# A hybrid encoder layer on one NeuronCore: new tables for the order of the instructions

## The chip, the cores and the metric

The kernel runs on 1 core of a Trainium2 chip. The core has five engines, each with an instruction stream of its own that it works off strictly in order: TensorE (PE in the rows: matmuls and transposes), VectorE (DVE), ScalarE (ACT), GpSimd (POOL) and SyncE (SP), which here only starts the DMAs. An engine whose next instruction waits for another engine stands still, with all that is queued behind that instruction.

The metric is the device time of one execution in microseconds (us). Lower is better.

## The reference

One encoder layer is computed for a prompt of 1024 frames and for the next 64 frames of a running stream that has a cache of 512 frames. Only the order of the operations matters here; all of it is float32.

```
z = x @ w_in                      # split into q,k,v,f of 6 FoX heads, u,v of the SGU, q,k,v of 6 stick-breaking heads
# A  FoX: causal softmax attention, logit += c_t - c_s with c = cumsum(log_sigmoid(f))
p = softmax(where(mask, q k^T / 8 + c_q - c_k, -1e30));  o_fox = p v
# B  SGU: 128-frame chunks, w_s lower triangular per channel group
u = gelu(u_g); v = layer_norm(gelu(v_g));  o_sgu = u * (w_s v + b_s)
# C  stick-breaking, strictly causal
a = exp(log_sigmoid(z) + sum of log_sigmoid(-z) over the later keys);  o_sb = a v
o = rms_norm_per_head(concat(o_fox, o_sgu, o_sb)) * g_mix
x = layer_norm(ALPHA * x + o @ w_out)
h = square(relu(x @ w_up));  y = layer_norm(ALPHA * x + h @ w_down)     # d_model 1024, d_ff 4096
```

The outputs are y for both groups and the new rows of the caches.

## The kernel before

**Matmuls in three passes.** A float32 matmul is made of three passes of a rounded type: each operand is split into a high part (a copy on ACT) and a low part (`lo_sub`, L215: source minus high part, on DVE or POOL), and `PASSES=((0,0),(0,1),(1,0))` multiplies high by high, high by low and low by high into one PSUM bank. Every tile that goes into a matmul therefore passes through ACT and then through DVE or POOL. Rows of L215 are such low parts, whatever the tile.

**Stage 1, to about 540 us: projection and attention.** `fill` makes the projections (L495, tiles kvfox, kvsb, sgv, sgu, qfox, qsb) and the SGU; `attn` makes the attention blocks. The build interleaves the two by a running cost. For a block of FoX heads the scores Sfox (L696) get the bias on DVE (L668) and the exponential on ACT. For stick-breaking the scores Ssb go through two sigmoids on ACT (L678, L679), a running product along the keys on DVE (L680, a scan of up to 1024 columns) and a product on POOL (L682, sgsb). PE transposes the rows (L744, ptfox and ptsb), ACT and DVE split them into high and low (pthfox, pthsb; L712 and L215), and PE multiplies them by v (L754 to L757, ofox and osb; L754 and L755 use the high part, L756 and L757 the low part). The SGU's v goes through a GELU (L893 to L896: ACT, DVE, ACT, DVE; tiles g1v and sgvv) and a LayerNorm (L967 to L973), and is mixed over 128 frames (L943, sgm). sgv and sgm share a ring of two PSUM banks, so a matmul of sgm waits until L896, the last reader of an older sgv, is done.

**Stage 2, to about 700 us:** the heads are normed (L316, L317), and the output projection (L373, mx) and the first LayerNorm follow; transposes (L1322, xta to xtd) make the MLP's operand xo.

**Stage 3, about 660 to 1000 us: x @ w_up** as a Winograd-like scheme: for each of 16 pieces p of w_up and for each of two column groups s (288 and 256 columns), seven products of 12 matmuls each (L1448) in four PSUM banks per s, zA, zB, zC and zD, three of the products in zA. After each product in zA, ACT copies the bank out (L1459, sn), and the next product into zA adds onto what is there; it has to wait for that copy. DVE makes the sums, relu and square (L1462 to L1492, hh), which go to DRAM. The weights are prepared beside it: load (wr), high parts (wa on ACT, L1386), low parts on POOL (L215), sums on DVE (L1395 to L1399), the sums' high parts on ACT (L1669, ws, two copies of 128x1024 for a piece) and low parts on DVE.

**Stage 4, from about 1000 us: h @ w_down** in the same scheme with 512 columns (L1913, banks A, B, D and p), the sums on DVE (L1878 and L1880, tiles acc), weights rd and wd split on ACT, POOL and DVE, and a LayerNorm at the end (L1982 to L2026).

**What sets the order.** The order in which an engine runs its instructions is not that of the code. At the end of `_build` (L2269 to L2283) a table for each of PE, ACT, DVE and POOL is read: a word `n+k` (n is 1 and k is 0 where left out) means n times "take the instruction with number k of those of this engine that are not yet taken". Each instruction taken gets an order dependency, without a semaphore, on the one taken before it. So a table is a permutation of the engine's instructions. SP has no table before: the order of its 672 DMAs comes from `in_order` helpers in a few places and from the scheduler.

Of the kernel before, what the change touches and what calls it, by code (L numbers as in the profile page):

```python
# [48 lines left out]
ORDER = {}  # L49
ORDER["PE"] = """  # L50
# [43 lines left out]
"""  # L94
ORDER["ACT"] = """
# [2208 lines left out]
```

## Time and profile before

| | |
|---|---|
| median of 3 runs | 1355.06 us (1354.13 to 1358.22) |
| profiled execution, its own time | 1357.01 us |
| profiled execution, span from first to last instruction | 1355.3 us |
| mean granted clock of TensorE | 0.991 of full speed |
| instructions | 24318 |
| PE busy | 1298.2 us, 96% of the span, 8827 matmuls and transposes |
| DVE / ACT / POOL busy | 1000.4 / 719.7 / 620.4 us |
| longest group on PE | 103.4 us, the output projection, 416 matmuls |

In the rows, a line reads: start, duration, engine, line of the code, operation, tile written <- tiles read (buffer numbers left out), shape, and in brackets the time that the engine stood idle before it and what ended that. Rows of a table by stretch give, for each engine, busy microseconds and the number of instructions in brackets, then the granted clock of TensorE and the use of the DMA engines. PE counts as busy while a matmul runs at half clock.

### The profile page before, as it was taken

The numbers are of one execution on the slowest core, as the hardware profiler recorded it, in microseconds if no ns is written. First come the engines' busy times: TensorE is split into PE (matmuls) and PEld (weight loads), VectorE is DVE, ScalarE is ACT, GpSimd is POOL, SyncE is SP. The second block draws the span as 40 slices with busy tenths as digits, with TensorE's granted clock in tenths as the row PEclk, the third lists the DMA queues.
The fourth block names the chain that finished last, engine by engine and source line by source line (L and its number), as shares of the span: only waits on it lengthen the run. The fifth ranks groups of instructions, "written<-read, shape, count | busy, mean of one in ns | idle before, by whom it ended". The sixth has DMA issues, their size and how long they took to land.

```text
span 1355.3 us, 24318 instructions
## 1 busy us (share of the span) xinstructions
PE 1298.2 (96%) x8827; PEld 1184.7 (87%) x8827; DVE 1000.4 (74%) x1797; ACT 719.7 (53%) x1561; POOL 620.4 (46%) x666
## 2 busy tenths in 40 slices
PE   7999999999999998999999999999999999999996
PEld 7898989999988997787899999999986888877774
DVE  4577666576888389779886777877687776767787
ACT  4366666576656376334523232232267676767665
POOL 3222222255675457666512221212186665655657
PEclk9999999999999998999999999999999999999998
DMA  7435565141403257432234444344568344434343
GB/s 230 110 117 149 157 201 146 53 101 44 101 16 77 63 180 260 147 117 70 79 120 143 157 139 160 127 153 149 189 231 280 125 143 149 144 121 160 102 140 132
DMA packets 158048, 185.64 MB, mean 137 GB/s; under 512 B 27740, under 2 KB 116124, under 8 KB 157928
## 3 DMA queue, kind: packets, MB, share of 16 engines
q1 hardware_dynamic: 155832, 183.01, 42.3%
q8 instruction: 70, 1.15, 0.4%
q10 hardware_dynamic: 2096, 1.07, 0.3%
q14 instruction: 50, 0.41, 0.1%
HBM read 117.65 MB, written 60.10 MB: 131 GB/s over the span
## 4 chain that ended last, share of the span: by engine, by line
PE 30%; DVE 8%; POOL 6%; DMA 5%; ACT 4%; issue 2%; SPq 0%; DVEq 0%; POOLq 0%; ACTq 0%
PE zA L1448 9%; PE zD L1448 6%; PE A L1913 4%; PE zB L1448 3%; PE zC L1448 3%; POOL wd L215 3%; PE D L1913 2%; DMA rd<-w_down 2%; POOL rd L1580 2%; PE mx L373 1%; DMA awa<-h_dr 1%; PE B L1913 1%; ACT wd L1386 1%; ACT st L1611 1%; DMA hs_dr<-hh 1%
## 5 line engine op out<-in xcount | busy, mean ns | idle before, releaser
L215 POOL TENSOR_TENSOR wa<-wr,wa 128x512 fp32r<-128x512 f32 x41 | 61.2, 1518 | 216.1 <-ACT wa L1386 216.1
L215 POOL TENSOR_TENSOR wd<-rd,wd 128x512 fp32r<-128x512 f32 x77 | 101.0, 1323 | 105.3 <-ACT wd L1386 68.1
L373 PE MATMUL mx<-xT,oTb 128*128 128x512 f32 (+1 forms) x416 | 103.4, 400 | 2.6 <-DVE oTb L215 2.4
L1448 PE MATMUL zD<-xo,ws 128*128 128x288 f32 (+1 forms) x720 | 95.2, 286 | 0.3 <-DVE hh L1462 0.3
L1448 PE MATMUL zA<-xo,ws 128*128 128x288 f32 (+1 forms) x720 | 95.0, 286 | 0.0
L373 PEld LDWEIGHTS mx<-xT,oTb 128*128 128x128 f32 (+1 forms) x416 | 75.7, 188 | 20.6 <-DVE oTb L215 3.7
L1448 PEld LDWEIGHTS zD<-xo,ws 128*128 128x128 f32 x720 | 91.5, 188 | 0.5 <-DVE hh L1462 0.5
L1448 PEld LDWEIGHTS zA<-xo,ws 128*128 128x128 f32 x720 | 91.4, 188 | 0.1
L495 PE MATMUL kvfox<-wkvfox,xT 128*128 128x256 f32 (+3 forms) x624 | 88.0, 289 | 3.2 <-ACT wkvfox L471 3.0
L1580 POOL TENSOR_TENSOR rd<-rd 128x512 f32<-128x512 f32 x56 | 79.2, 1415 | 23.8 <-DVE b L215 21.5
L1386 ACT ACTIVATE wd<-rd 128x512 fp32r<-128x512 f32 x105 | 63.6, 623 | 45.9 <-POOL rd L1580 23.9
L495 PE MATMUL kvsb<-wkvsb,xT 128*128 128x256 f32 (+1 forms) x624 | 87.2, 285 | 0.2 <-ACT wkvsb L471 0.2
L682 POOL TENSOR_TENSOR sgsb<-sgsb,snsb 128x127 f32<-128x127 f32 (+7 forms) x48 | 59.5, 1242 | 57.9 <-DVE snsb L680 47.8
L1913 PE MATMUL A<-wd,wd 128*128 128x512 f32 x312 | 82.4, 393 | 2.4 <-DVE acc L1880 1.9
L495 PEld LDWEIGHTS kvfox<-wkvfox,xT 128*128 128x128 f32 (+1 forms) x624 | 79.5, 190 | 4.7 <-ACT wkvfox L471 3.4
L680 DVE TENSOR_TENSOR_SCAN snsb<-snsb,one 128x128 f32<-128x128 f32 (+7 forms) x48 | 72.0, 1502 | 10.9 <-ACT snsb L679 9.3
L495 PEld LDWEIGHTS kvsb<-wkvsb,xT 128*128 128x128 f32 (+1 forms) x624 | 78.2, 187 | 0.6 <-ACT wkvsb L471 0.4
L1913 PEld LDWEIGHTS A<-wd,wd 128*128 128x128 f32 x312 | 57.8, 188 | 17.9 <-DVE acc L1880 4.3
L1459 ACT ACTIVATE sn<-zA 128x256 f32<-128x256 f32 (+1 forms) x80 | 30.9, 388 | 68.4 <-PE zA L1448 60.9
L1913 PE MATMUL A<-wd,h4a 128*128 128x512 f32 x240 | 64.1, 392 | 1.8 <-DVE acc L1880 1.0
L1669 ACT ACTIVATE ws<-wr 128x1024 fp32r<-128x1024 f32 x28 | 29.1, 1056 | 64.3 <-DVE wr L1398 64.3
L1386 ACT ACTIVATE wa<-wr 128x512 fp32r<-128x512 f32 x42 | 23.5, 622 | 61.6 <-DMA wr<-w_up 57.7
(551 smaller groups left out, 3765.7 us busy)
## 6 DMA issues: line engine op xcount, KB each, us to landing
h_dr<-hh SPq DMA_DIRECT2D x30, 512.0 KB, 3.2
rd<-w_down SPq DMA_DIRECT2D x30, 512.0 KB, 4.5
wr<-w_up SPq DMA_DIRECT2D x13, 1024.0 KB, 5.5
hr<-h_dr SPq DMA_DIRECT2D x31, 384.0 KB, 4.1
h_dr<-hh SPq DMA_DIRECT2D x30, 384.0 KB, 3.6
raw<-w_in SPq DMA_DIRECT2D x44, 256.0 KB, 3.2
wo_dr<-swo SPq DMA_DIRECT2D x32, 256.0 KB, 2.3
xT<-wo_dr SPq DMA_DIRECT2D x8, 1024.0 KB, 7.9
```

Of the source, the lines that this page charges most:

```text
L215: eng.tensor_tensor(out, src, hi.bitcast(F32), op=ALU.subtract)
L373: nc.tensor.matmul(acc[0:m], oT[:, k, hx, 0:m], wo[k // 4][hw][:, k % 4, cs], start=(i == 0), stop=(i == len(seq) - 1))
L495: nc.tensor.matmul(acc[0:n, c0:c0 + n1 - n0], xT[k // 4][:, k % 4, c:c + n], wt[:, k, hw, n0:n1], start=(i == 0), stop=(i == len(seq) - 1))
L680: nc.vector.tensor_tensor_scan(g[:, 0:n][:, ::-1], g[:, 0:n][:, ::-1], one.broadcast_to([P, n]), 1.0, op0=ALU.mult, op1=ALU.bypass)
L682: nc.gpsimd.tensor_tensor(s[:, 0:n - 1], s[:, 0:n - 1], g[:, 1:n], op=ALU.mult)
L1386: nc.scalar.activation(hi, raw, AF.Copy)
L1448: nc.tensor.matmul(z, w[:, hw, k], xop(s, bo, hx)[:, k, :], start=(new and k == 0 and j == 0), stop=(k == 3 and j == 2), skip_group_check= ...
L1459: nc.scalar.activation(c, z, AF.Copy)
L1580: eng.tensor_tensor(r[:, o], r[:, x], r[:, y], op=ALU.subtract)
L1611: nc.scalar.activation(st, t[:, 0, q].bitcast(F32), AF.Copy)
L1669: nc.scalar.activation(ws[:, 0, q, c], src[:, q], AF.Copy)
L1913: nc.tensor.matmul(z, h[:, hx, q, o], wset[self.c % 2][q][:, hw, wb], start=((n in (0, 3) or n == 1 and self.c == 0) and q == 0 and j == 0 ...
```

## The change

The tables of PE, ACT, DVE and POOL are replaced by others, a table for SP is added, and the loop that reads them takes SP too and leaves out instructions that only mark a boundary. Nothing else changes: each engine has the same instructions with the same operands, and SP's new table gives the same order of DMAs as before. The new tables add 88 lines, so that L1448 before is L1536 after, L215 is L303, L896 is L984, and lines from L163 on shift alike. The number of runs of equal rows in PE's order goes from 2939 to 4166: the new order changes between tiles more often.

```diff
 ORDER["PE"] = """
-9 8+23 55 +8 8+25 +8 14 4+34 2+10 45 4+1 7+13 1 +12 4+36 12 4+24 14 2+36 19 15+1 8 8+24 24 +8 8 8+1 9 8+1
...
++4 2 2+2 4 2+23 +25 4+23 12 4+12 2+32 +11 2+31 6 +5 +24 2+5 +51 2 +20 2+51 7+3 2+13 3 +39 +36 8 +10 2 +25 +51
...
+ORDER["SP"] = """
++9 +4 1 +20 +38 1 2+39 +4 +6 +37 +8 +36 +38 +263 4 2+14 10 2+4 4 4+19 1 4+1 +10 2+1 6 2+38 1 +2 1 6+1 4 +2 1
...
-    for eng, e in (("PE", nc.tensor), ("ACT", nc.scalar), ("DVE", nc.vector), ("POOL", nc.gpsimd)):
-        left = [i for i in traced[from_here:] if i.engine == e.engine]
+    for eng, e in (("PE", nc.tensor), ("ACT", nc.scalar), ("DVE", nc.vector), ("POOL", nc.gpsimd), ("SP", nc.sync)):
+        left = [i for i in traced[from_here:] if i.engine == e.engine and "Boundary" not in type(i).__name__]
         prev = None
         for word in ORDER[eng].split():
             n, k = (int(x or d) for x, d in zip(re.match(r"(\d*)\+?(\d*)", word).groups(), (1, 0)))
```

Three places show what the new tables do. The names carry the block and a running number: sgvv5 is the SGU's v of row tile 5, zA2_0 is bank A for weight piece 2 and column group 0.

The first is on DVE, near 400 us, where the SGU and stick-breaking run side by side. Before:

```order
L680 SCALAR_TENSOR_TENSOR snsb1_5_1_5694<-snsb1_5_1_5694,one_70 128x768
L971 TENSOR_SCALAR sgvv4_5777<-sgvv4_5777,sgst4_5783 128x256
L894 SCALAR_TENSOR_TENSOR g1v5_5819<-g1v5_5819,sgv5_5793 128x256
L972 TENSOR_TENSOR sgvv4_5777<-sgvv4_5777,gvb_5432 128x256
L896 TENSOR_TENSOR sgvv5_5818<-g1v5_5819,sgv5_5793 128x256
L215 TENSOR_TENSOR pthsb1_2_0_2_5713<-ptsb1_2_0_2_5709,pthsb1_2_0_2_5713 128x384
```

After, from the same scan to the same split (L303 is L215 before, L768 is L680, L982 is L894, L1059 is L971, L984 is L896, L1060 is L972):

```order
L768 SCALAR_TENSOR_TENSOR snsb1_5_1_5694<-snsb1_5_1_5694,one_70 128x768
L982 SCALAR_TENSOR_TENSOR g1v5_5819<-g1v5_5819,sgv5_5793 128x256
L1059 TENSOR_SCALAR sgvv4_5777<-sgvv4_5777,sgst4_5783 128x256
L984 TENSOR_TENSOR sgvv5_5818<-g1v5_5819,sgv5_5793 128x256
L1060 TENSOR_TENSOR sgvv4_5777<-sgvv4_5777,gvb_5432 128x256
L303 TENSOR_TENSOR pthsb1_2_0_2_5713<-ptsb1_2_0_2_5709,pthsb1_2_0_2_5713 128x384
```

The GELU's two steps for tile 5 (g1v5 and sgvv5) have each moved ahead by one LayerNorm step of tile 4.

The second is on DVE, near 532 us, in the last stick-breaking block, from its scan to the second low part of its rows. Before:

```order
L680 SCALAR_TENSOR_TENSOR snsb2s_7666<-snsb2s_7666,one_70 128x576
L997 TENSOR_TENSOR up6_7231<-up6_7231,sgu7_1_7685 128x256
L316 TENSOR_REDUCE ss0_7568<-sq0_7566 128x8
L894 SCALAR_TENSOR_TENSOR g1u5_7629<-g1u5_7629,up4_7162 128x256
L317 SCALAR_TENSOR_TENSOR ss0_7568<-ss0_7568,rge_7560 128x8
L215 TENSOR_TENSOR pthsb2_3_1_0_7700<-ptsb2_3_1_0_7695,pthsb2_3_1_0_7700 128x512
L997 TENSOR_TENSOR up8_7262<-up8_7262,sgu8_1_7732 64x256
L316 TENSOR_REDUCE ss0_7568<-sq0_7566 128x8
L776 TENSOR_REDUCE otsb2_3_0_7703<-otpsb2_3_0_7704 128x2x64
L502 TENSOR_TENSOR up8_7262<-up8_7262,sgu8_1_7732 64x256
L215 TENSOR_TENSOR pthsb2_3_1_1_7713<-ptsb2_3_1_1_7708,pthsb2_3_1_1_7713 128x512
```

After (L404 is L316, L405 is L317):

```order
L768 SCALAR_TENSOR_TENSOR snsb2s_7666<-snsb2s_7666,one_70 128x576
L404 TENSOR_REDUCE ss0_7568<-sq0_7566 128x8
L405 SCALAR_TENSOR_TENSOR ss0_7568<-ss0_7568,rge_7560 128x8
L303 TENSOR_TENSOR pthsb2_3_1_0_7700<-ptsb2_3_1_0_7695,pthsb2_3_1_0_7700 128x512
L404 TENSOR_REDUCE ss0_7568<-sq0_7566 128x8
L982 SCALAR_TENSOR_TENSOR g1u5_7629<-g1u5_7629,up4_7162 128x256
L405 SCALAR_TENSOR_TENSOR ss0_7568<-ss0_7568,rge_7560 128x8
L303 TENSOR_TENSOR pthsb2_3_1_1_7713<-ptsb2_3_1_1_7708,pthsb2_3_1_1_7713 128x512
```

The up6 product has moved behind, g1u5 from ahead of pthsb2_3_1_0 to between it and pthsb2_3_1_1, and the up8 steps and the reduction of otsb2_3_0 behind both.

The third is on PE, in stage 3, from the end of the second product of piece 2 in zA2_0 to its third. Before:

```order
L1448 MATMUL zA2_0_9410<-xo0_8042,ws2_9350 128x288 x12
L1448 MATMUL zA2_1_9424<-xo13_8811,ws2_9350 128x256 x12
L1448 MATMUL zD2_0_9492<-xo0_8042,ws2_9350 128x288 x12
L1448 MATMUL zD2_1_9505<-xo14_8810,ws2_9350 128x256 x12
L1448 MATMUL zA2_0_9410<-xo0_8042,ws2_9350 128x288 x12
```

After:

```order
L1536 MATMUL zA2_0_9410<-xo0_8042,ws2_9350 128x288
L1536 MATMUL zC2_1_9560<-xo13_8811,wa2_9261 128x256
L1536 MATMUL zA2_0_9410<-xo0_8042,ws2_9350 128x288
L1536 MATMUL zC2_0_9546<-xo0_8042,wa2_9261 128x288
L1536 MATMUL zD2_0_9492<-xo0_8042,ws2_9350 128x288
L1536 MATMUL zA2_0_9410<-xo0_8042,ws2_9350 128x288 x2
L1536 MATMUL zD2_0_9492<-xo0_8042,ws2_9350 128x288 x2
L1536 MATMUL zC2_0_9546<-xo0_8042,wa2_9261 128x288
L1536 MATMUL zD2_0_9492<-xo0_8042,ws2_9350 128x288 x2
L1536 MATMUL zC2_0_9546<-xo0_8042,wa2_9261 128x288
L1536 MATMUL zA2_0_9410<-xo0_8042,ws2_9350 128x288 x12
L1536 MATMUL zA2_1_9424<-xo13_8811,ws2_9350 128x256 x2
```

Before, whole products of 12 matmuls lie between the second and the third product in zA2_0, 36 matmuls in all; after, products are cut into short runs, and 6 matmuls lie between them.

Elsewhere the moves are of the same kind and size: tiles of PE's order move by a few microseconds of PE's work, in stage 3 by up to nine. In stage 4, at about 1030 us, DVE's second split of wd1_0 moves behind the sums of D1_0 and A1_1, and the sum of A1_0 ahead of that of p11_0. At about 431 us, DVE's split pthsb1_3_0_3 moves ahead of g1v8 (L894). Near 57 us, PE's first scores Sfox2 move behind projection matmuls of kvfox1_1 and qfox2_2.

More of the change, by code (lines that the diff above doesn't have):

```diff
@@ L50 @@
 ORDER["PE"] = """
[43 rows of a table removed]
[104 rows of a table added]
 """
 ORDER["ACT"] = """
[25 rows of a table removed]
[31 rows of a table added]
 """
 ORDER["DVE"] = """
[31 rows of a table removed]
[36 rows of a table added]
 """
 ORDER["POOL"] = """
[6 rows of a table removed]
[11 rows of a table added]
+"""
+ORDER["SP"] = """
[9 rows of a table added]
 """
```

294 rows, old and new, of the table ORDER are left out of this document.

## The prediction

> **What bounds the kernel now.** I read the page's busy line first, then the stretches, then the chain of work, then PE's waits, and last what DVE and ACT were doing at those waits.
>
> ```profile
> PE 1298.2 (96%) x8827; PEld 1184.7 (87%) x8827; DVE 1000.4 (74%) x1797; ACT 719.7 (53%) x1561; POOL 620.4 (46%) x666
> PE 30%; DVE 8%; POOL 6%; DMA 5%; ACT 4%; issue 2%; SPq 0%; DVEq 0%; POOLq 0%; ACTq 0%
> ```
>
> PE is busy for 1298.2 of 1355.3 us, and no other engine exceeds 74%. An order changes no amount of work, so what it can win or lose is PE's idle 57.1 us and the time that PE ran at half clock. In the chain that ended last, PE leads with 30%, and DVE (8%), POOL (6%) and DMA (5%) follow. By stretches (length, busy us of PE, its weight loads, DVE, ACT, POOL, then granted clock and DMA):
>
> ```profile
> 0.00:700.00 700.00, 660.88 (x4953) 618.76 (x4954) 508.95 (x1030) 388.19 (x920) 324.07 (x427) 0.99 0.41 121
> 700.00:1000.00 300.00, 300.00 (x2423) 299.12 (x2423) 225.11 (x340) 93.84 (x179) 70.68 (x47) 1.00 0.46 154
> 1000.00:1355.30 355.30, 337.37 (x1454) 266.79 (x1452) 266.32 (x429) 237.68 (x463) 225.62 (x193) 0.99 0.45 154
> ...
> 70.00:74.40 4.40, 3.94 (x22) 3.82 (x21) 3.85 (x12) 3.21 (x10) 1.04 (x2) 0.61 0.67 179
> 401.00:406.00 5.00, 3.98 (x19) 3.53 (x20) 3.42 (x10) 3.82 (x9) 2.94 (x5) 0.66 0.13 28
> 432.00:437.00 5.00, 4.91 (x28) 4.61 (x29) 3.81 (x10) 3.69 (x9) 2.39 (x4) 0.66 0.58 130
> 534.00:543.00 9.00, 7.54 (x32) 6.42 (x33) 8.65 (x18) 4.11 (x9) 7.31 (x7) 0.62 0.98 369
> ```
>
> Of the idle time 39.1 us lie before 700 us, none between 700 and 1000, and 17.9 after. So stage 3 has nothing to give and can only lose. The last four rows show the clock: length times (1 minus clock) is 1.7, 1.7, 1.7 and 3.4 us, 8.5 us of work lost.
>
> The large waits on PE (in brackets the idle time and what ended it):
>
> ```profile
> 4.44 0.87 PE L451 MATMUL xtp<-ident,xr 128*128 128x128 f32 x3 [4.44 <-DMA xr<-x_prompt]
> 57.00 0.58 PE L696 MATMUL Sfox<-kpfox,qdfox 128*128 128x128 f32 x3 [1.67 <-DMA qdfox<-qdfox]
> 401.50 0.38 PE L943 MATMUL sgm<-vh,wst 128*128 128x256 f32 x1 [1.75 <-DVE sgvv L896]
> 431.92 0.33 PE L756 MATMUL osb<-pthsb,vpsb 128*128 128x128 f32 x1 [1.67 <-DVE pthsb L215]
> 534.62 0.38 PE L756 MATMUL osb<-pthsb,vpsb 128*128 128x256 f32 x1 [2.25 <-DVE pthsb L215]
> 1029.66 0.96 PE L1913 MATMUL A<-wd 128*128 128x512 f32 x3 [1.23 <-DVE acc L1878]
> 1032.03 0.94 PE L1913 MATMUL A<-wd,h4a 128*128 128x512 f32 x3 [0.72 <-DVE acc L1880]
> 1034.00 0.49 PE L1913 MATMUL D<-wd 128*128 128x512 f32 x1 [1.04 <-DVE acc L1878]
> ...
> 1343.63 1.07 PE L1913 MATMUL A<-wd,wd 128*128 128x512 f32 x4
> ```
>
> PE is late at single places, and mostly for DVE. The last row ends at 1344.70, so 10.6 us at the end are a tail without PE.
>
> **The change part by part.** It removes and adds no instruction; all the terms are waits.
>
> *Near 400 us (sgm).* DVE before:
>
> ```profile
> 398.68 0.75 DVE L971 TENSOR_SCALAR sgvv<-sgvv,sgst 128x256 f32<-128x256 f32 x1
> 399.35 0.41 DVE L894 SCALAR_TENSOR_TENSOR g1v<-g1v,sgv 128x256 f32<-128x256 f32 x1
> 399.68 1.43 DVE L972 TENSOR_TENSOR sgvv<-sgvv,gvb 128x256 f32<-128x256 f32 x1
> 401.04 0.41 DVE L896 TENSOR_TENSOR sgvv<-g1v,sgv 128x256 f32<-128x256 f32 x1
> ```
>
> sgm waits for a bank until L896 ends at 401.45. With L894 first, at 398.68, ACT's sigmoid runs beside L971, and L896 starts when L894 (0.33 to the next start) and L971 (0.67) are through, at 399.7 instead of 401.04: 1.34 us off a wait of 1.75. I take −1.3, with an end at −0.9 for what ACT's step may take longer than L971. L972 comes 0.3 us later; its result is copied to vh and is needed only for a later sgm, so that costs nothing. If the sum for tile 4 is late after all, that cost is under 0.4 us.
>
> *Near 431 us.* DVE before:
>
> ```profile
> 430.46 0.94 DVE L894 SCALAR_TENSOR_TENSOR g1v<-g1v,gsv 64x256 f32<-64x256 f32 x1
> 431.32 0.54 DVE L215 TENSOR_TENSOR pthsb<-ptsb,pthsb 128x384 fp32r<-128x384 f32 x1
> ```
>
> The split moves ahead of g1v8: −0.86 (431.32 less 430.46). PE's table also puts seven short matmuls of Ssb and ptsb ahead of the waiting pair, which cover the rest: −1.6 in all, and −0.9 if those seven would have run anyway without waiting.
>
> *Near 534 us.* DVE before:
>
> ```profile
> 531.85 0.39 DVE L997 TENSOR_TENSOR up<-up,sgu 128x256 f32<-128x256 f32 x1
> 532.16 0.67 DVE L316 TENSOR_REDUCE ss<-sq 128x8 f32<-128x512 f32 x1
> 532.76 0.86 DVE L894 SCALAR_TENSOR_TENSOR g1u<-g1u,up 128x256 f32<-128x256 f32 x1
> 533.55 0.41 DVE L317 SCALAR_TENSOR_TENSOR ss<-ss,rge 128x8 f32<-128x8 f32 x1
> ```
>
> L997 (0.31 to the next start) and L894 (0.79) leave the stretch ahead of pthsb2_3_1_0: −1.1. g1u5 now stands ahead of the next split, where up8 and the reduction of otsb have left, so that one is no later.
>
> *Near 57 us.* PE's Sfox2 waits 1.67 for a DMA. The new table puts projection matmuls whose inputs are there ahead of it, more than the wait is long: −1.7 (0 if the DMA, itself released by DVE, comes later too).
>
> *Near 1030 us.* The sum of A1_0 goes ahead of that of p11_0, and the second split of wd1_0 behind two sums. Of the waits 1.23, 0.72 and 1.04 the first loses 0.67 and the third up to all of its 1.04. The second stands behind the first split in both. I take −1.5, ends −0.7 and −2.0. The split that is now late feeds a later product.
>
> The five make −7.2, with ends −4 and −9.
>
> *The clock.* Half clock shows just after the waits of 1.75, 1.67 and 2.25 us at 401, 431 and 534 us. One wait's length alone doesn't decide: the equal one of 1.67 at 57 us left the clock whole, and the dip at 70 us follows shorter waits close together.
>
> ```profile
> 57.00:65.00 8.00, 8.00 (x66) 8.00 (x67) 2.64 (x5) 0.76 (x2) 2.23 (x4) 1.00 0.36 107
> 68.00:71.00 3.00, 1.79 (x12) 1.53 (x12) 2.97 (x13) 2.85 (x9) 1.28 (x1) 0.99 0.19 44
> ```
>
> If the three waits shrink as above, I expect 1.7 + 1.7 us and half of the 3.4 at 534 to come back: −5.1, with ends 0 and −8.5. [...]
>
> *The other waits.* Idle time of 57.1, less the start (4.4), the tail (10.6) and the five places (1.67 + 1.75 + 1.67 + 2.25 + 2.99 = 10.3), leaves 31.8 us in many small waits. The moves there are of the same kind, but not all can go. These two, for instance, keep their place behind the same work on DVE:
>
> ```profile
> 186.45 0.74 PE L696 MATMUL Sfox<-kpfox,qdfox 128*128 128x256 f32 x4 [1.58 <-DVE mfox L668]
> 662.10 0.63 PE L1322 MATMUL xtc<-ident,y 128*128 128x128 f32 x4 [1.41 <-DVE xr L1342]
> ```
>
> I take a third, −10, with ends 0 and −32.
>
> *The tail.* The 10.6 us after the last matmul are one LayerNorm on DVE, ACT and POOL. The new table puts two steps of an earlier tile's LayerNorm on DVE behind the last sum there. I take 0, with an end at +1.5.
>
> *New waits, above all in stage 3.*
>
> ```profile
> 699.81 0.64 PE L1448 MATMUL zA<-xo,ws 128*128 128x256 f32 x4
> 700.28 1.58 PE L1448 MATMUL zD<-xo,ws 128*128 128x256 f32 x12
> 701.70 1.58 PE L1448 MATMUL zA<-xo,ws 128*128 128x256 f32 x12
> ...
> 700.48 0.38 ACT L1459 ACTIVATE sn<-zA 128x256 f32<-128x256 f32 x1 [2.44 <-PE zA L1448]
> ...
> L1669 ACT ACTIVATE ws<-wr 128x1024 fp32r<-128x1024 f32 x28 | 29.1, 1056 | 64.3 <-DVE wr L1398 64.3
> L1459 ACT ACTIVATE sn<-zA 128x256 f32<-128x256 f32 (+1 forms) x72 | 27.7, 388 | 61.0 <-PE zA L1448 53.5 <-ACT wa L1386 2.3 <-DVE hh L1468 1.6
> L1386 ACT ACTIVATE wa<-wr 128x512 fp32r<-128x512 f32 x39 | 21.8, 622 | 58.7 <-DMA wr<-w_up 57.7 <-PE zC L1448 1.0
> ```
>
> Between two uses of a zA bank lie at least the 12 matmuls of one product here, 1.42 us; the copy starts 0.03 us after the bank is written and takes 0.39. With 6 matmuls between, as in piece 2 after the change, it is 6 x 0.118 = 0.71 us, and 0.29 us is to spare as long as ACT is free. A copy that meets one of the 28 weight copies of 1.06 us on ACT makes PE late by up to 0.77. None such and 28 are the ends, 0 and +22. Few of the reuses are that close, and I take a quarter, 7 waits of about 1 us with what they cost elsewhere: +7.
>
> The sum: −7.2 − 5.1 − 10 + 0 + 7 = −15.3 against the profiled execution, whose own time of 1357.0 is 2 us above the median of 1355.06. From the median: 1340.
>
> **The rivals.**
>
> 1. *Slower: stage 3 pays for its short runs.* The profile has PE without any idle time for 300 us there, with whole products between reuses. If all 28 weight copies (0.77 each) and the 39 of wa (0.62, less the 0.29, so 0.33 each) come in front of an awaited zA copy, it costs 22 + 13 = 35 us against −22.3 of gains (7.2 + 5.1 + 10): 1355 + 13 = 1368. From 22.3 + 4 us of new waits on the kernel is slower. For it: ACT is in order, and its wa copies wait for DMAs (57.7 us). Against it: ACT is busy for only 93.84 of those 300 us.
>
> 2. *No change: DVE and POOL bound the early stretches.*
>
> ```profile
> 350.00:400.00 50.00, 47.35 (x391) 45.85 (x389) 44.88 (x88) 31.34 (x86) 35.12 (x49) 1.00 0.24 62
> ```
>
> Where DVE is busy for 44.88 of 50 us, a split that is moved ahead makes another late, and PE meets that one next. Then the gains are the waits near 57 and 1030 us, 3 us, less new waits of 3 us: 1355. Against it: in 0 to 700 us as a whole DVE is busy for 73%.
>
> 3. *The clock stays.* Without the term of 5.1: 1345. For it: the dip at 70 us needed no long wait, and the new order makes many short ones. Against it: three of the four dips stand right behind the longest waits.
>
> 4. *A large gain.* Nearly all waits before the tail go: 57.1 − 4.4 − 10.6 = 42 us and the clock's 8.5, three quarters of them 38: 1317.
>
> **How the numbers follow.** The forecast 0.42; rival 1 0.23; rival 2 0.11; rival 3 0.12; rival 4 0.12. Faster is the forecast with rivals 3 and 4, 0.66. About 4 us, 0.3%, is what a measurement of this kernel can tell from no change. The forecast's own range, from its term for small waits (0 or −20) and for new ones (0 or +14), one at its end at a time, is 1330 to 1350. The range over all reaches from 1314, just below rival 4, to 1364, a little below what rival 1 gives; I leave out about 0.05 below and 0.14 above.
>
> **What would show it.** If I am right, the waits at 57, 401, 432, 534 and 1034 us are under 0.7 us or gone, the clock row shows no slice under 1.00 between 350 and 500 us, PE's idle time before 700 us falls from 39 to about 22 us, and stage 3 shows a few waits of PE on `sn` from ACT, 7 us in all. I am wrong if stage 3's PE idle time is over 20 us, if the same splits on DVE are waited for as long at other matmuls, or if PE takes longer for the same matmuls in short runs with no wait in the trace.

## The result, and the profile after

The changed kernel takes 1348.27 us (median of 7 runs, 1347.59 to 1349.55) against 1355.06 us (median of 7, 1351.49 to 1358.22): a ratio of 0.9954, with an interval of 0.994 to 0.9968. It is faster by 0.5%, a little under 7 us, where 15 were forecast.

The page of the changed kernel (busy time by engine, then shares of the chain that ended last), and TensorE's part of the stretches:

```profile
PE 1295.9 (96%) x8827; PEld 1185.0 (88%) x8827; DVE 1007.4 (75%) x1797; ACT 724.8 (54%) x1561; POOL 619.4 (46%) x666
...
PE 70%; DVE 14%; DMA 6%; ACT 4%; issue 3%; POOL 2%; SPq 0%; DVEq 0%; ACTq 0%; POOLq 0%
```

```profile
0.00:700.00 700.00, 669.33 (x5045) 626.13 (x5046) 516.50 (x1042) 394.83 (x924) 320.13 (x427) 1.00 0.42 123
700.00:1000.00 300.00, 293.90 (x2333) 290.98 (x2332) 226.07 (x331) 94.83 (x181) 77.09 (x50) 1.00 0.45 149
1000.00:1345.90 345.90, 332.64 (x1453) 267.93 (x1451) 264.80 (x426) 235.17 (x457) 222.21 (x190) 0.99 0.46 158
```

The span went from 1355.3 to 1345.9 us. PE's idle time fell from 39.1 to 30.7 us before 700 us, rose from 0 to 6.1 in 700 to 1000, and fell from 17.9 to 13.3 after that. By 700 us the core had done 5045 matmuls instead of 4953; by 1000 us it had done 7378 against 7376. What the first half won, stage 3 had nearly used up.

PE's waits of the changed kernel, by what was waited for (total us, times, longest):

```profile
PE zA L1536 <- ACT sn L1547: 7.9, 5, 5.2
PE xtp L539 <- DMA xr<-x_prompt: 4.5, 1, 4.5
PE kvfox L583 <- ACT wkvfox L559: 2.7, 1, 2.7
PE zD L1536 <- DVE hh L1550: 2.5, 3, 1.0
PE pkcsb L901 <- DVE kc_sb L303: 1.7, 1, 1.7
PE kvfox L583 <- DVE qdfox L735: 1.6, 1, 1.6
PE qsb L724 <- DVE gsv L590: 1.5, 1, 1.5
PE mx L461 <- DVE y L468: 1.4, 1, 1.4
...
PE osb L844 <- DVE pthsb L303: 0.9, 3, 0.3
```

The longest group before was

```profile
PE osb L756 <- DVE pthsb L215: 7.6, 8, 2.2
```

and is down to 0.9. First now is zA behind ACT's copy sn, which PE never waited for before, and 5.2 of its 7.9 us are a single wait.

Since a matmul has the same name in both kernels, and each is known by its place in PE's order, one can say how far PE is ahead of the kernel before once it has done the same amount of work. This table is worked out from the starts of the matmuls in the traces (us ahead of the profiled execution of before; work in us of matmuls at full clock; the runs e1 to e7 are told below):

```
work done          600    650    900    last matmul
                 (~667) (~726) (~986)  (the time in the changed kernel)
changed kernel    17.9    9.6    1.6    10.6
e1                18.1   16.7    9.6    18.1
e2                17.3   17.7   17.7    16.4
e3                18.0   18.4   16.3    24.2
e4                 0.3   -7.4   -7.4    -6.9
e5                 1.5    1.8    2.5     3.2
e6                15.8    7.3   -0.4     8.7
e7                15.0    6.3   -6.4     2.4
```

So the new order wins 17.9 us up to the start of stage 3, loses 8.3 in one stretch of 60 us, loses 8.0 more over the rest of stage 3, and wins 9.0 in stage 4. The tail after the last matmul is 1.2 us longer.

**The one place.** PE, ACT and SP of the changed kernel near 676 us:

```profile
676.14 1.09 PE L1536 MATMUL zA<-xo,ws 128*128 128x288 f32 x3 [5.16 <-ACT sn L1547]
```

```profile
665.23 2.25 ACT L1757 ACTIVATE ws<-y 128x1024 fp32r<-128x1024 f32 x2
675.68 0.41 ACT L1547 ACTIVATE sn<-zA 128x288 f32<-128x288 f32 x1 [8.20 <-DMA h_dr<-y]
```

```profile
671.97 0.32 SPq L1581 DMA_DIRECT2D h_dr<-y  x1
672.43 0.34 SPq L1582 DMA_DIRECT2D h_dr<-y  x1
```

The copy that PE waits for is the first one out of zA1_0. ACT itself stood idle for 8.20 us ahead of it, and not for PE: it waited until a transfer out of a tile y had landed. The tiles y are row buffers that are used again here, for weights and, as y7 is, for the results of the first product chain. A copy into sn has nothing to do with y7's data. The two share memory. In the built programs the allocations can be compared: of 2150 tiles, 500 lie at another address in the changed kernel, although no line of the allocation was touched: the ring buffers for rows and in PSUM are handed out by the order of the work. So the operands are the same by name, and not by place. Before, y7 lay at byte 88192 of the partition; after, it lies at 100480 to 104576, and sn1_0 starts at 103104 in both.

Behind the wait the clock is at half (busy us and granted clock of the changed kernel, as in the rows by stretch):

```profile
673.02:676.43 3.41, 0.29 (x1) 0.29 (x2) 2.40 (x7) 0.41 (x1) 0.00 (x0) 0.50 0.71 279
676.43:679.85 3.42, 3.42 (x16) 3.42 (x16) 0.00 (x0) 0.00 (x0) 0.00 (x0) 0.50 0.98 258
```

### The profile page after: what moved, and what is told of

Its sections match the earlier page's. It is cut to its first block, busy times and chain, and to the rows that moved or that the text cites. A ratio compares the mean times of both kernels' runs of the same rounds, so it can differ in the third digit from the quotient of the medians.

```text
span 1345.9 us, 24239 instructions
## 1 busy us (share of the span) xinstructions
PE 1295.9 (96%) x8827; PEld 1185.0 (88%) x8827; DVE 1007.4 (75%) x1797; ACT 724.8 (54%) x1561; POOL 619.4 (46%) x666
## 4 chain that ended last, share of the span: by engine, by line
PE 70%; DVE 14%; DMA 6%; ACT 4%; issue 3%; POOL 2%; SPq 0%; DVEq 0%; ACTq 0%; POOLq 0%
PE A L2001 10%; PE zA L1536 7%; PE mx L461 6%; PE kvsb L583 5%; PE zD L1536 5%; PE D L2001 5%; PE kvfox L583 4%; PE zC L1536 2%; PE B L2001 2%; PE zB L1536 2%; PE qfox L724 2%; PE qsb L724 2%; PE Sfox L784 2%; PE Ssb L784 1%; PE ptfox L832 1%
## 5 line engine op out<-in xcount | busy, mean ns | idle before, releaser
L303 POOL TENSOR_TENSOR wa<-wr,wa 128x512 fp32r<-128x512 f32 x41 | 63.9, 1579 | 238.4 <-ACT wa L1474 238.4
L303 POOL TENSOR_TENSOR wd<-rd,wd 128x512 fp32r<-128x512 f32 x77 | 103.8, 1355 | 114.8 <-ACT wd L1474 109.7
L1536 PE MATMUL zA<-xo,ws 128*128 128x288 f32 (+1 forms) x720 | 113.2, 289 | 7.9 <-ACT sn L1547 7.9
L1536 PE MATMUL zD<-xo,ws 128*128 128x288 f32 (+1 forms) x720 | 116.4, 288 | 3.4 <-DVE hh L1550 2.5
L1536 PEld LDWEIGHTS zA<-xo,ws 128*128 128x128 f32 x720 | 99.2, 189 | 9.1 <-ACT sn L1547 9.1
L1536 PEld LDWEIGHTS zD<-xo,ws 128*128 128x128 f32 x720 | 99.7, 189 | 4.9 <-DVE hh L1550 3.4
L583 PE MATMUL kvfox<-wkvfox,xT 128*128 128x256 f32 (+3 forms) x624 | 96.3, 294 | 4.3 <-ACT wkvfox L559 2.7
L583 PE MATMUL kvsb<-wkvsb,xT 128*128 128x256 f32 (+1 forms) x624 | 93.2, 288 | 0.0
L768 DVE TENSOR_TENSOR_SCAN snsb<-snsb,one 128x256 f32<-128x256 f32 (+7 forms) x48 | 69.6, 1456 | 6.2 <-ACT snsb L767 4.1
L2001 PE MATMUL A<-wd,h4a 128*128 128x512 f32 x240 | 69.7, 391 | 0.9 <-ACT h4a L1695 0.6
L2001 PEld LDWEIGHTS A<-wd,wd 128*128 128x128 f32 x312 | 58.5, 188 | 13.3 <-DVE acc L1968 0.7
L1536 PE MATMUL zB<-xo,wa 128*128 128x288 f32 (+1 forms) x360 | 65.9, 288 | 0.0
L1536 PE MATMUL zC<-xo,wa 128*128 128x288 f32 (+1 forms) x360 | 62.9, 287 | 0.0
```

The costliest lines, as they stand in the source:

```text
L303: eng.tensor_tensor(out, src, hi.bitcast(F32), op=ALU.subtract)
L583: nc.tensor.matmul(acc[0:n, c0:c0 + n1 - n0], xT[k // 4][:, k % 4, c:c + n], wt[:, k, hw, n0:n1], start=(i == 0), stop=(i == len(seq) - 1))
L768: nc.vector.tensor_tensor_scan(g[:, 0:n][:, ::-1], g[:, 0:n][:, ::-1], one.broadcast_to([P, n]), 1.0, op0=ALU.mult, op1=ALU.bypass)
L1536: nc.tensor.matmul(z, w[:, hw, k], xop(s, bo, hx)[:, k, :], start=(new and k == 0 and j == 0), stop=(k == 3 and j == 2), skip_group_check= ...
L2001: nc.tensor.matmul(z, h[:, hx, q, o], wset[self.c % 2][q][:, hw, wb], start=((n in (0, 3) or n == 1 and self.c == 0) and q == 0 and j == 0 ...
```

## The experiments

Theory A says: the order wins before stage 3 about what was forecast; stage 3 loses by this overlap and by its own short runs.

**e1: the overlap taken away.** The changed kernel with another layout of stage 3's buffers:

```diff
-for tag, n in (("wr", 2048), ("wa", 3072), ("hh1", 2048), ("sn1", 768), ("sn0", 768), ("hh0", 2304), ("ws", 4096),
+for tag, n in (("wr", 2048), ("sn0", 768), ("hh0", 2304), ("wa", 3072), ("hh1", 2048), ("sn1", 768), ("ws", 4096),
```

> The new order, with one thing changed: in the buffers of stage 3 the tiles sn0 and hh0 lie at the start, behind wr, so that the first copy out of zA1_0 no longer lands on the memory of y7, whose transfer to DRAM it waits for. Theory A (the 5.16 us wait at 676 us comes from that overlap of buffers): the wait goes, with the half clock behind it (0.93 over 50 us, 1.7 us lost), so 1348.3 - 6.9 = 1341. Rival B (the copy is late because it stands behind two weight copies of 1.1 us on ScalarE): the wait stays at 2 us or more and the time is over 1345.

Measured: 1341.83 us (6 runs), 0.9913 of before, interval 0.9892 to 0.9935; the changed kernel beside it on the same chip took 1348.14 (ratio 0.9962, 0.9948 to 0.9975). ACT in e1, the same copy:

```profile
665.02 2.26 ACT L1757 ACTIVATE ws<-y 128x1024 fp32r<-128x1024 f32 x2
669.62 0.41 ACT L1547 ACTIVATE sn<-zA 128x288 f32<-128x288 f32 x1 [2.34 <-PE zA L1536]
```

It stands behind the same two weight copies and now waits only for PE's product. The 5.16 us wait is gone, and no stretch of half clock is left before the last matmul (from 0 to 1330 us the granted clock is 1.00 in each stage). Rival B is out: 6.3 us of the missing gain come back with the other layout. That it is the overlap, and no other effect of that layout, e4 checks from the other side.

**e2: the new order, then the old one.** All four tables were rewritten: first, in the new order, what the changed kernel starts before 652 us; then the rest in the old order. The layout is that of e1.

> The new order for everything that the changed kernel started before 652 us, and the old order for all the rest, with the buffers as in the run with sn elsewhere. Theory A (the new order wins 18 us before stage 3 and loses in stage 3 by its own short runs and the one overlap): stage 3 has under 1 us of idle time, and the time is 1355 - 17 = 1338. Rival C (stage 3 is held by something that does not depend on its order, so an earlier start is given back: weights, transfers): TensorE waits 8 us or more in stage 3 and the time is 1346 or more.

**e3: new, old, new.** The same, and what the kernel before starts after 985 us again in the new order.

> As the run before it, and the new order again for what the old kernel started after 985 us. Theory A with stage 4 winning 8 us by its order: 1338 - 8 = 1330. Rival D (stage 4 gains only because it starts from a TensorE that was late, and the other engines had caught up): no gain over the run before it, 1337 to 1339.

Measured: e2 1341.07 us (0.991, interval 0.9887 to 0.9932), e3 1334.59 us (0.9859, interval 0.9836 to 0.9883). The stretch of e2 from 700 to 950 us:

```profile
700.00:950.00 250.00, 250.00 (x2038) 249.86 (x2037) 190.07 (x285) 71.81 (x134) 56.24 (x38) 1.00 0.43 143
```

With the old order stage 3 has no idle time, and e2 keeps its lead of 17.7 us all through it: nothing holds stage 3 that doesn't depend on its order, and rival C is out. The times are 3 and 5 us above the expected 1338 and 1330, which were reckoned from a before of 1355; beside these runs it took 1352.5. e3 is 6.5 us faster than e2, so stage 4's gain belongs to its order, and rival D is out. e3 beats both kernels, the changed one by 13.6 us.

Where the changed kernel loses stage 3's other 8 us can be read from the trace of e1, which has the overlap no more: eight waits of 0.34 to 1.25 us, 5.8 in all, as these of the changed kernel,

```profile
710.62 1.72 PE L1536 MATMUL zD<-xo,ws 128*128 128x288 f32 x11 [1.05 <-DVE hh L1550]
743.30 2.13 PE L1536 MATMUL zA<-xo,ws 128*128 128x256 f32 x15 [0.88 <-ACT sn L1547]
```

some behind weight work that stands ahead of the sum or copy on its engine, some only because hardly a matmul lies between two products in one bank; and some 2 us of pace: from 700 to 950 us, counting only steps under 150 ns, a matmul with 256 columns is followed by the next after 115.9 ns on average within a run and 116.1 where the tile changes, against 113.9 in the kernel before. As the steps are longer within the runs too, it isn't the change of tile itself that costs; the cause stays open.

**e4: the overlap put into the old kernel.** The kernel before with the buffers in the order wr, hh0, sn0, wa, hh1, sn1, ws, by which sn1_0 comes to lie on its y7.

> The kernel before, with the buffers of stage 3 laid out so that sn0 lies on the memory of y7 (in the old order y7 is at another place, and the layout is another one for that). Theory A (the wait comes from the overlap and needs no new order): the first copy out of zA1_0 now waits for y7's transfer, TensorE stands for 6 to 9 us near 690 us, and the kernel takes 5 to 10 us longer than before. Rival B (only the new order's weight copies make that copy late): no change, within 2 us.

Measured: 1360.24 us (12 runs), 1.0053 of before, interval 1.0034 to 1.0073: 6 us slower than before (1354.1). PE and ACT near 690 us:

```profile
693.82 3.25 PE L1448 MATMUL zA<-xo,ws 128*128 128x288 f32 x12 [6.51 <-ACT sn L1459]
```

```profile
693.35 0.41 ACT L1459 ACTIVATE sn<-zA 128x288 f32<-128x288 f32 x1 [7.62 <-DMA h_dr<-y]
```

The overlap makes the wait in the old order too.

**e5: the three moves on VectorE alone.** The kernel before, with the moves of DVE that the prediction costed at 401, 431 and 534 us, and no other change of the tables (built, 92 tiles get another address and two DMAs change places):

```diff
 L680 snsb1_5_1
-L971 sgvv4
 L894 g1v5
-L972 sgvv4
+L971 sgvv4
 L896 sgvv5
+L972 sgvv4
...
-L894 g1v8
 L215 pthsb1_3_0_3
+L894 g1v8
...
-L997 up6 <- sgu7_1
-L894 g1u5          (two rows on, behind L316)
 L215 pthsb2_3_1_0
+L894 g1u5
...
 L215 pthsb2_3_1_1
+L997 up6 <- sgu7_1
```

> The kernel before, with only VectorE's moves at 401, 431 and 534 us (g1v5 and sgvv5 ahead of the LayerNorm steps of tile 4; pthsb1_3_0_3 ahead of g1v8; up6 and g1u5 behind pthsb2_3_1_0). Theory A (the prediction's terms): waits -1.3, -0.9 and -1.1, and three stretches of half clock of 1.7 us gone, -8 in all. Rival E (clock stays): -3. Rival F (VectorE's work is the bound there, the next split is late): within 1.5 us of before.

**e6: the changed kernel with the same three moves undone.**

> The changed kernel with those three moves of VectorE undone. Theory A: +3 us of waits and up to +5 by half clock, 1351 to 1356. Rival G (TensorE's new order covers those waits by itself): under +1.5 us.

Measured: e5 1354.21 us, a ratio of 1.0002 (interval 0.9983 to 1.002): nothing. e6 1351.89 us, 0.9986 of before (0.9967 to 1.0006), 3.7 us above the changed kernel's 1348.2. That kernel was measured in another round: as ratios to the kernel before beside them the two are 0.9986 and 0.9962, with intervals that overlap, and in the traces e6 is 1.9 us behind the changed kernel at the last matmul. PE's waits in e5 (its lines are one less than those of before):

```profile
399.90 0.50 PE L942 MATMUL sgm<-vh,wst 128*128 128x256 f32 x2 [0.34 <-DVE sgvv L895]
401.45 0.33 PE L755 MATMUL osb<-pthsb,vpsb 128*128 128x128 f32 x1 [0.93 <-DVE pthsb L214]
404.67 0.44 PE L812 MATMUL pkcsb<-ident,cache_sb_k 128*128 128x128 f32 x2 [1.23 <-DVE otsb L775]
...
430.15 0.33 PE L755 MATMUL osb<-pthsb,vpsb 128*128 128x128 f32 x1 [0.81 <-DVE pthsb L214]
...
534.37 0.39 PE L755 MATMUL osb<-pthsb,vpsb 128*128 128x256 f32 x1 [1.66 <-DVE pthsb L214]
...
537.28 0.38 PE L755 MATMUL osb<-pthsb,vpsb 128*128 128x256 f32 x1 [1.00 <-DVE pthsb L214]
```

The three waits shrink as costed, from 1.75 to 0.34, from 1.67 to 0.81 and, less, from 2.25 to 1.66. But PE then meets DVE's next outputs: 0.93 and 1.23 us within 5 us of the first place, where the second had been 0.52, and 1.00 instead of 0.78 at the third. That is rival F: without a new order on PE, DVE is the bound there. Reckoned as in the table above, e5 is 1.3 us slower than before over PE's work from 350 to 550 us. In the new order the same moves are worth 2.6 us of lead over those stretches (e6). The changed kernel gains 7.0 us there in all, so most of it comes from what the new tables put beside them. That it is PE's order above all is likely, and no run takes that order alone.

**e7: no table for SP.** The changed kernel, with SP left out of the loop that reads the tables.

> The changed kernel without SP's table: the scheduler then issues some DMAs in another order (stores and loads change places by a few). Theory: the DMA queue has room (42% of its engines' time), loads are issued far ahead, so within 2 us of the changed kernel. Rival: a load comes behind a waiting store, and TensorE waits for it, 3 us or more slower.

Measured: 1355.72 us (12 runs), a ratio of 1.0013 (0.9998 to 1.0029) to before, 7.5 us slower than the changed kernel was in its own round (ratio 0.9962, 0.9948 to 0.9975). The expectation missed. The lead lost shows at 460 to 510 us (3 us) and above all in stage 3 (some 5 us more than in the changed kernel), as here, where the changed kernel waits 0.43 us:

```profile
886.50 1.44 PE L1536 MATMUL zD<-xo,ws 128*128 128x288 f32 x9 [2.10 <-DVE hh L1550]
```

The way back from this wait leads to a transfer again. DVE's sum waited for ACT, and ACT's copy into hh for a store of that buffer's older contents:

```profile
885.55 0.41 ACT L1547 ACTIVATE hh<-zA 128x288 f32<-128x288 f32 x1 [3.59 <-DMA h_dr<-hh]
885.99 0.46 DVE L1550 TENSOR_TENSOR hh<-zD,hh 128x288 f32<-128x288 f32 x1 [1.98 <-ACT hh L1547]
909.59 0.41 ACT L1547 ACTIVATE hh<-zA 128x288 f32<-128x288 f32 x1 [5.36 <-DMA h_dr<-hh]
```

Behind the second of these copies PE stands 1.13 us. In the changed kernel ACT has only the first of these two waits, and it is 1.91 us long:

```profile
881.11 0.41 ACT L1547 ACTIVATE hh<-zA 128x288 f32<-128x288 f32 x1 [1.91 <-DMA h_dr<-hh]
```

The rival of the expectation named a load behind a waiting store; here it is the store itself that is late. So without the table that only repeats the order of DMAs, the other four tables gain nothing that can be measured. The two programs differ in 193 of 672 places in the order of the DMAs and in the addresses of 31 tiles. Which of these makes the stores land later, or costs the 3 us at 460 to 510 us, was not tried.

## Why the prediction was right or wrong

**The direction and the early stages: right in sum.** Up to stage 3 the terms were 1.7, 1.3, 1.6 and 1.1 for the places, 5.1 for the clock and most of the 10 for small waits; 17.9 came. The waits at 57, 401, 431 and 534 us are gone, as the prediction asked, and no stretch between 350 and 500 us is at half clock. But other matmuls now wait about as long nearby: 1.57 us at 52, 1.50 at 412, 1.69 at 506 and 1.36 at 586 us. In its parts the working was off, and that the sum came out so near is partly luck. About 8 of the 17.9 us are won ahead of 390 us, where the prediction names only the 1.7 at 57 us. The clock gave more: the 17.1 us of half clock that the profile of before shows ahead of the last matmul, 8.5 us of work, are all gone from there. The three DVE terms were worth less by themselves: e5 shows that the mechanism, a split moved ahead, does end that wait, but the step "−1.3 ... −1.6 ... −1.1" counted a wait as won without asking what PE meets next on a DVE that is busy for 45 of 50 us. They count only together with the rest of the new tables.

**Stage 4: too small.** −1.5 was costed at 1030 us; stage 4 gained 9.0 up to the last matmul. About 4 of these came near 1030 us and most of the rest after 1290 us, where before had waits of 0.41, 0.31, 0.37 and 1.20 us and the changed kernel has none above 0.25. In the prediction these were part of the small waits. The tail's +1.2 lies inside its bounds, where the sum took 0.

**The step that failed: "It removes and adds no instruction; all the terms are waits", and with it the +7 for new waits in stage 3.** Stage 3's short runs cost 8.0, near the 7 that stood for them, and e2 shows that it is the order alone. That the size fits is luck in part: the term priced waits for sn copies, and in the changed kernel these are 2.8 us from 700 to 1000 us; waits for DVE's hh are 3.3, and the 2 us of pace have no wait in the trace, which the prediction had named as a sign of being wrong. The term also left something out. A new order also gives 500 tiles another address, and where a pool laid over older buffers meets a tile that is still being sent out, an instruction waits for data it never reads. That cost 8.3 us of lead, 5.16 as the wait and most of the rest as half clock behind it (e1 gets 7.0 back). Nothing in the working looked at addresses; the overlap stood in the sum at nothing. Over the whole span the sum of the traces is −17.9 + 8.3 + 8.0 − 9.0 + 1.2 = −9.4 against the −15.3 of the forecast: waits and clock gave 26.9 instead of 22.3, and the overlap alone took more back than that. With the overlap removed, e1's 1341.8 is near the forecast's 1340, but before took only 1352.5 beside it: the gain there is 10.6 us of the 15.

**Rivals.** The slower rival had the right place and about a quarter of its price: 8 us of the 35. The rival of no change describes e5, the three moves alone, and not the new order, which won 17.9 us before stage 3. The clock rival ("stays") is wrong for the new order, where the half clock at 401, 431 and 534 us is gone with the waits of 1.75, 1.67 and 2.25 us ahead of it. But in e5 shorter waits did not bring the clock back: half clock still begins at 431.84 and 537.65 us, with the waits there at 0.81 and 1.66 us. The large gain did not come, in e3 neither.

**Against the medians.** The traces differ by 9.4 us, the medians by 6.8: the profiled execution of before lies 2.0 us above its median, and the changed kernel's 0.7 below its own. Before scatters more, 1348.6 to 1360.9 us over 35 runs, than the changed kernel, 1346.0 to 1350.9 over 12. In e4 and e5, which keep the old order nearly everywhere, the profiled executions (granted clock 0.987 and 0.989) show 30.7 and 23.9 us of half clock, partly at places where before shows none (at 186 to 189 us and at 1026 to 1033). So the half clock differed between these executions, but run by run it explains little of the scatter: over the 35 runs of before, time and granted clock have a correlation of only −0.34 (1351.59 us came at a clock of 0.989, 1356.84 us at 0.994). What makes the rest is open.

## What to carry to other kernels

An order is never only an order: where buffers are handed out by the order of the work, it also decides which memory each tile gets (500 of 2150 tiles moved here), so after a reordering, compare the addresses and look for an engine that waits for a transfer of data that it doesn't use (ACT for 8.20 us here, and PE for 5.16 behind it); the repair can be one line of layout. A wait taken off one place is won only if the releasing engine has nothing else to deliver soon after; ask for the next two waits on it before counting it (in e5 1.75 us shrank to 0.34, and 0.93 and 1.23 followed). And take a reordering apart by stages: where one stage has no idle time (stage 3 before: PE busy for 300.00 of 300 us), a new order has no wait left to win, and old and new orders can be joined at a cut (1334.6 us here, against 1348.1 for the changed kernel and 1352.5 for the one before).

## What the runs showed of the hardware

In the profile of the kernel before, half clock shows four times ahead of the last matmul: for 3.41 us each from 70.92, 402.01 and 432.73 us, and for 6.83 us from 535.13. In the 3.41 us ahead of these, PE was idle for 1.36, 1.75, 1.87 and 2.25 us. In the profile of the changed kernel it shows once there, for 6.83 us from 673.02, and PE was idle for 2.04 of the 3.41 us ahead. Two pairs of stretches of the kernel before:

```profile
429.30:432.72 3.42, 1.55 (x12) 1.11 (x11) 3.31 (x6) 1.55 (x5) 2.18 (x3) 1.00 0.27 63
432.72:436.13 3.41, 3.32 (x17) 3.02 (x16) 2.56 (x7) 2.18 (x7) 1.83 (x3) 0.50 0.44 104
53.90:57.31 3.41, 1.74 (x16) 1.57 (x15) 3.25 (x7) 0.60 (x2) 1.45 (x1) 1.00 0.51 122
57.31:60.72 3.41, 3.41 (x31) 3.41 (x30) 2.33 (x5) 0.11 (x1) 1.18 (x2) 1.00 0.16 44
```

In the first pair PE is busy for 1.55 us, and the next stretch runs at 0.50; in the second it is busy for 1.74, and the next one runs at full clock. In each pair a wait of 1.67 us lies whole within the first stretch. At 431 us shorter gaps bring the idle time to 1.87 us; at 57 us the wait is all of it. So of two waits of 1.67 us one was followed by 3.41 us at half clock, which is 1.7 us of work, and the other by none. The idle time doesn't sort these places either: 1.36 us of it came ahead of half clock at 70.92 us, and 1.67 us ahead of full clock at 57.31. What decides is not shown by these runs.
